# Pool waits tile by tile, the first mLSTM inputs on GpSimd's queue, and modulation tiles behind cells and evacuations

## The chip, the cores and the metric

The kernel runs on one core of one Trainium2 chip. The metric is the device time of one execution in microseconds. Three executions of the kernel before took 1891.66, 1893.18 and 1893.83 us; the median is 1893.18.

## The reference

One layer of a diffusion trunk is computed in float32 for 128 context tokens and 512 latent tokens, 640 in all, with a model width of 1024:

```python
def layer(x, mods, l, p, ctx):
    hh = rmsnorm(x, g[0]) * (1 + m[1]) + m[0]
    x = x + 0.5 * m[2] * swiglu(hh, p['ffn1_w1'][l], p['ffn1_w3'][l], p['ffn1_w2'][l])
    hh = rmsnorm(x, g[1]) * (1 + m[4]) + m[3]
    y, ctx_out = token_mixer(hh, p, l, ctx)
    x = x + m[5] * y
    hh = rmsnorm(x, g[2]) * (1 + m[7]) + m[6]
    x = x + 0.5 * m[8] * swiglu(hh, p['ffn2_w1'][l], p['ffn2_w3'][l], p['ffn2_w2'][l])
...
def token_mixer(h, p, l, ctx):
    mq, mk, mv, mo, mg, dq, dk, dv, gm, gd = split_cols(h @ p['w_in'][l])
    ...
    att = diff_attention(q_att, keys, vals, lam)
    ...
    h_f, st_f = mlstm_chunkwise(q, k, v, log_i[0], log_f[0], st0_f)
    h_b, st_b = mlstm_chunkwise(rev(q), rev(k), rev(v), ...)
    hm = (h_f + rev(h_b)).transpose(0, 2, 1, 3)
    hm = (rmsnorm(hm, p['g_mh'][l]).reshape(B, T, ML_WIDTH) * jax.nn.sigmoid(mo))
    y = jax.nn.sigmoid(gm) * (hm @ p['w_br_m'][l]) + jax.nn.sigmoid(gd) * (att @ p['w_br_d'][l])
    out = y @ p['w_out'][l]
```

The nine modulation vectors `m[j]` are columns of `silu(c) @ w_ada + b`. The attention has 8 heads, the mLSTM 4 heads of 256, in 5 chunks of 128 tokens and two directions; its state `C` starts at zero for the context chunk and from an input for the latent chunks.

## The kernel before, in words

Activations lie feature by feature: a tile holds 128 features by 640 tokens. A product of full precision is made of three matmuls on halves: a weight tile `raw` (128x2048, 1 MB) is cast by ScalarE (ACT) to a high part `wH` (L123), VectorE (DVE) subtracts to make the low part `wL` (L39, from `split_into`), and TensorE (PE) multiplies wH and wL with the high and low parts of the activations (`hH`/`hL` or `aHL`). A unit of such a product is 24 matmuls of 128x320 into one PSUM tile `ps_p`, followed by an evacuation; a granule is the four units of one weight tile.

The program runs through five stages: the first feed-forward; attention with the projections, interleaved; the mLSTM; the two branch products; the output product with the second feed-forward. The change touches the third and fourth, and the pools from the second on.

**Pools.** A `tile_pool` takes a stretch of SBUF or PSUM, and a later pool may take the same stretch. By default, the first tile of the later pool waits for everything that lay in the stretch. With `reuse_waits="tile"` each tile waits for what lay at its own addresses.

**mLSTM.** `Memory.load` fetches, per head, `va` (values, 640 KB), two halves of `P` (stabilisers, 320 KB each, one per direction, to which DVE adds `mask`), and `load_c` the two states `C`. `prep` makes token-major keys `mktok` (ACT, from PE's transposes), takes the exponentials of P on ACT (ten of 128x128 a head) and multiplies P by the scores `ps_st` on DVE. `cell` then does the chunk's products on PE (`ps_n`, `ps_u`), scales values to `wv`, updates `C` (or `Cn` for the context), and ends with `reciprocal` of `den` and, where the second direction is added, with `hs`. `gate` fetches `so` and applies a logarithm and an exponential to it (L1650, L1651 of the code below). `finish` normalises and transposes `hs` and multiplies it into `so`. Head h+1 is loaded and prepared among the cells of head h. Projections for the branch gates (evacuated to `stage` and written to `gm_dram`, `gd_dram`) and, at head 3, the splits of the attention output into `aHL` from `a_raw` stand between the cells.

**Branches.** Four granules of `w_brd` multiply `aHL`; `d_evac` multiplies a unit by a sigmoid `sig` into `y1`. Head 3's `finish` and the split of `zT_dram` (tiles `z_raw`, three at a time) into `hH`/`hL` stand among them. Four granules of `w_brm` then multiply those, and `m_evac` adds y1 and splits the sum into `yH` and `yL`. `x` comes back from `x_dram` by four transfers of 640 KB for the residual.

**Modulation tiles.** 23 of the columns of the modulation are still to be made in these stages, by `Columns`: `fetch` loads a weight column `raw_a` (512 KB), `tile` runs two multiply-and-sum passes over it on DVE (L671, printed as ISA in the order; 128x1024 each) against `csil`.

**One ring for all.** Weight tiles, `a_raw`, `z_raw` and `raw_a` share the pool `rawp` under one tag with two buffers. A load takes one of the two and waits until what lay there has been read for the last time: by wL's subtraction for a weight, by the second pass for a `raw_a`, by the last hL for a `z_raw`.

**What sets the order.** PE runs in program order, and so do the loads made by `load` (L74), which SyncE (SP) issues. The other instructions are placed by a scheduler, engine by engine, and each engine and queue then runs its list from front to back: an instruction that waits holds up everything behind it. `tc.issue_after(x)` makes what is written inside stand behind x. Most loads are issued by SP; the queue of GpSimd (POOL) is otherwise used for the feed-forwards.

The splits share one line, L39, and all matmuls one line, L52 (`mm`), so the rows of the profile are told apart by the tiles' names.

Of the kernel before, what the change touches and what calls it, by code (L numbers as in the profile page):

```python
# [31 lines left out]
def tile_trunk(ctx: ExitStack, tc: tile.TileContext, a: dict):  # L32
# [977 lines left out]


    att = ExitStack()
    ap = att.enter_context(tc.tile_pool(name="att", bufs=1))
    psum = att.enter_context(tc.tile_pool(name="ps2", bufs=5, space=PSUM))
    ps_s = att.enter_context(tc.tile_pool(name="ps2s", bufs=1, space=PSUM))

    fill = Fill()

# [376 lines left out]
            nc.sync.dma_start(out=dst[:, 2 * g + mt, half(hf)], in_=t)  # L1395
        return f

    with tc.tile_pool(name="gates", bufs=1) as gt:
# [20 lines left out]
    k_pool = ctx.enter_context(tc.tile_pool(name="mlk", bufs=1, side="right"))  # L1419
    queries_of = ExitStack()  # L1420
    q_pool = queries_of.enter_context(tc.tile_pool(name="mlq", bufs=1, side="right"))
# [111 lines left out]


    cs = ExitStack()
    cs_p = cs.enter_context(tc.tile_pool(name="csil", bufs=1, side="right"))
    csil = cs_p.tile([128, 2, D], F32, name="csil")
    for v in range(2):
        nc.sync.dma_start(out=csil[:, v, :], in_=csil_dram[v].partition_broadcast(128))
# [6 lines left out]
    columns.place(23, csil, load_columns, 0)  # L1546

    ml = ExitStack()
    mp = ml.enter_context(tc.tile_pool(name="ml", bufs=1))
    psum = ml.enter_context(tc.tile_pool(name="ps3", bufs=8, space=PSUM))  # L1550
    mask = load(mp, [128, 2, 128], a["mask"], name="mask")

    fill.pace(1.4, 1)
    for g in range(1, 4):
# [4 lines left out]
    class Memory:  # L1559
# [4 lines left out]

        def load(self):
            h = self.h
            self.va = mp.tile([128, 5, 258], F32, tag="va", name="va", bufs=2)
            nc.sync.dma_start(out=self.va[:, :, 0:256], in_=v_dram[h])
            vec.memset(self.va[:, :, 256:257], 1.0)
            vec.memset(self.va[:, :, 257:258], 0.0)  # L1570
            self.P = mp.tile([128, 5, 2, 128], F32, tag="P", name="P", bufs=2)
            for d in range(2):
                nc.sync.dma_start(
                    out=self.P[:, :, d, :], in_=nm_dram[32 * d + h].partition_broadcast(128).rearrange("p (c t) -> p c t", c=5)
                )
                tt(vec, self.P[:, :, d, :], self.P[:, :, d, :], mask[:, d, None, :].to_broadcast([128, 5, 128]), ALU.add)
            self.ktok = mp.tile([128, 5, 256], F32, tag="ktok", name="mktok", bufs=2)
            self.hs = mp.tile([128, 5, 256], F32, tag="hs", name="hs", bufs=2)

        def load_c(self):  # L1580
            self.C = [load(mp, [128, 2, 258], a["c_aug"][d, self.h], tag=f"C{d}", name="C", bufs=2) for d in range(2)]

        def prep(self, i):

# [15 lines left out]
        def cell(self, i, d, accumulate, inter, update):  # L1600

            h = self.h
            hd = 4 * d + h
            va, hs, C = self.va, self.hs, self.C[d]
            p1 = psum.tile([128, 512], F32, tag="mm", name="ps_n1")
            p1 = p1[:, :258]
            mm(p1, self.P[:, i, d, :], va[:, i, :], start=True, stop=True)
            tok = slice(i * 128, (i + 1) * 128)
            num = p1
            if inter:  # L1610
                p2 = psum.tile([128, 512], F32, tag="mm", name="ps_n2")
                p2 = p2[:, :258]
                for dt in range(2):
                    mm(p2, mqT[h][:, dt, tok], C[:, dt, :], start=dt == 0, stop=dt == 1)
                num = mp.tile([128, 258], F32, tag="num", name="num", bufs=3)
                act(num, p2, AF.Copy, scale=cols[:, i, 2, hd : hd + 1])
                tt(vec, num, p1, num, ALU.add)
            if update:
                wv_ = mp.tile([128, 258], F32, tag="wv", name="wv", bufs=2)
                act(wv_, va[:, i, :], AF.Copy, scale=cols[:, i, 1, hd : hd + 1])  # L1620
                if inter:
                    new = mp.tile([128, 2, 258], F32, tag=f"C{d}", name="C", bufs=2)
                else:
                    new = mp.tile([128, 2, 258], F32, tag="N", name="Cn", bufs=1)
                for dt in range(2):
                    p3 = psum.tile([128, 512], F32, tag="mm", name="ps_u")
                    p3 = p3[:, :258]
                    mm(p3, self.ktok[:, i, dt * 128 : (dt + 1) * 128], wv_, start=True, stop=True)
                    if inter:
                        stt(new[:, dt, :], C[:, dt, :], decay[:, 32 * d + h, i : i + 1], p3, ALU.mult, ALU.add)  # L1630
                    else:
                        act(new[:, dt, :], p3, AF.Copy)
                if inter:
                    self.C[d] = new
                else:
                    nc.sync.dma_start(out=a["new_c"][d, h], in_=new)
            den = mp.tile([128, 1], F32, tag="den", name="den", bufs=4)
            ts(den, num[:, 256:257], cols[:, i, 3, hd : hd + 1], ALU.max)
            stt(den, num[:, 256:257], -1.0, den, ALU.mult, ALU.max)
            vec.reciprocal(den, den)  # L1640
            if accumulate:
                stt(hs[:, i, :], num[:, 0:256], den, hs[:, i, :], ALU.mult, ALU.add)
            else:
                act(hs[:, i, :], num[:, 0:256], AF.Copy, scale=den)

# [60 lines left out]
    for h in range(4):  # L1706
        m = mem[h]
        later = [[] for _ in range(10)]
        if h < 3:
            mem[h + 1].load()  # L1710
            for i in range(5):
                later[3 + i].append(lambda i=i: mem[h + 1].prep(i))
        if h > 0:
            for i in range(5):
                later[4 + i].append(lambda i=i: mem[h - 1].finish(i))
        if h == 3:
            for k in range(KT):
                later[2 + k].append(attended)
        later[9].append(m.gate)
        steps = [(s, 0, s >= 2, True, s < 3) if d == 0 else (3 - s, 1, s >= 2, True, s < 3) for s in range(4) for d in range(2)]  # L1720
        steps += [(4, d, d == 1, False, True) for d in range(2)]
        for st, then in zip(steps, later):
            if st[0] == 4 and st[1] == 0 and h < 3:
                mem[h + 1].load_c()
            m.cell(*st)
            for f in then:
                f()
            fill.slot(0)
            if len(box_ml) % 4 == 0:
                columns.fetch(1)  # L1730
            elif len(box_ml) % 4 == 2:
                columns.tile()
            box_ml.append(0)
        m.stats()
    fill.drain()
# [13 lines left out]
    def d_evac(g):  # L1749
        def f(p, mt, hf):  # L1750
            t = gate_of(gd_dram, g, mt, hf, pool=mp, tag=("ktok", "P", "va", "hs")[g], bufs=2)
            tt(vec, y1[g][:, mt, half(hf)], p, t, ALU.mult)
        return f

    for g in range(4):
# [1 line left out]
    for i in range(5):  # L1757
        fill.one()
        mem[3].finish(i)
        columns.fetch((i + 1) % 2)  # L1760
        if i % 2:
            columns.tile()
    for k in range(6):
        if k % 3 == 0:
            raw = load(rawp, [128, 3, T], zT_dram[:, k : k + 3, :], tag="raw", name="z_raw")
# [14 lines left out]

    psum = Banks(ctx.enter_context(tc.tile_pool(name="ps4", bufs=1, space=PSUM)))
    tmp = ctx.enter_context(tc.tile_pool(name="tmp", bufs=1))
    out = ExitStack()
    zp = out.enter_context(tc.tile_pool(name="yy", bufs=1))
    x_pairs = pairs("k", "x")
    x = [x_pairs[d // 2][:, d % 2, :] for d in range(KT)]
    with tc.tile_pool(name="gate", bufs=1) as gp:
        yH, yL = hh_tiles(zp)
        yHL = [(yH[:, k], yL[:, k]) for k in range(KT)]

        def m_evac(g):
            def f(p, mt, hf):
# [3 lines left out]
                tt(vec, t, t, y1[g][:, mt, cs], ALU.add)  # L1796
                d = 2 * g + mt
                act(yH[:, d, cs], t, AF.Copy)
                tt(vec, yL[:, d, cs], t, yH[:, d, cs].bitcast(F32), ALU.subtract)
            return f  # L1800

        for g in range(4):
# [2 lines left out]
            nc.sync.dma_start(out=x_pairs[g], in_=x_dram[:, 2 * g : 2 * g + 2, :])  # L1805
# [219 lines left out]
```

## Time and profile before

| what | value |
|---|---|
| median of three executions | 1893.18 us |
| the profiled execution | 1891.94 us |
| its span in the profile | 1890.2 us |
| mean granted clock of PE | 0.986 |
| busy: PE, DVE, ACT, POOL | 1816.4, 1299.5, 847.0, 32.9 us |

The span is 1.74 us shorter than the execution it belongs to, and the median is 1.24 us above that execution. A row of the timeline gives the start and duration in microseconds, engine, line, operation, written tile and read tiles; repeated instructions are drawn together (x10), and in brackets stands the idle time ahead of the first and what ended it. "SPq" is the queue of issues on SP: the duration of such a row is that of issuing, not of the transfer. A row of the chain of waits has start, duration and what the span's end waited for in it. Rows of windows have the busy time and the count of instructions of each engine, and then the granted clock of PE ("PEclk"), the share of DMA and its rate.

### The profile page before, as it was taken

The page shows a single profiled execution, that of the slowest core. Times are in us where ns is not written, and L with a number is a line of the kernel's source. Part 1 is how long each engine was busy: PE and PEld are TensorE (multiplying, and loading weights), DVE is VectorE, ACT ScalarE, POOL GpSimd, SP SyncE. Part 2 cuts the span into 40 slices and gives each one's busy share as a digit, 9 for nine tenths or more (in the row PEclk, how much of TensorE's full clock was granted, in tenths as well). Part 3 has the DMA queues.
Part 4 walks back from the last instruction along what each step waited for, and adds up shares of the span by engine and source line. Part 5 has one row for each costly group of instructions (what it writes and reads, how often), then busy time and mean ns, then how long its engine had stood idle before and what let it go on. Part 6 is the DMA issues. An engine that isn't in the chain of part 4 may idle for free.

```text
span 1890.2 us, 30782 instructions
## 1 busy us (share of the span) xinstructions
PE 1816.4 (96%) x12658; PEld 1778.2 (94%) x12658; DVE 1299.5 (69%) x2193; ACT 847.0 (45%) x1447; POOL 32.9 (2%) x51
## 2 busy tenths in 40 slices
PE   6999999999989999999999989999999899999989
PEld 4999999999889999999999978899899899999989
DVE  7888885575787665754745457757666778886575
ACT  5644453112553354543543455663336555554232
POOL 1000001100000000000000000000000000000000
PEclk9999999999999999999999989999999999999999
DMA  8344449953325222221221255554742435547952
GB/s 325 119 165 163 154 149 330 323 190 118 116 88 174 100 76 80 73 98 51 84 93 59 98 194 166 191 196 162 266 155 80 150 126 184 185 172 269 336 193 91
DMA packets 127438, 299.82 MB, mean 159 GB/s; under 512 B 9473, under 2 KB 90625, under 8 KB 114625
## 3 DMA queue, kind: packets, MB, share of 16 engines
q1 hardware_dynamic: 118642, 259.07, 39.3%
q0 software_dynamic: 8656, 38.80, 5.6%
q8 instruction: 99, 1.62, 0.3%
q14 instruction: 41, 0.34, 0.1%
HBM read 234.20 MB, written 63.63 MB: 158 GB/s over the span
## 4 chain that ended last, share of the span: by engine, by line
PE 79%; DVE 9%; DMA 7%; ACT 3%; issue 2%; SPq 0%; DVEq 0%; ACTq 0%
PE ps_f L52 41%; PE ps_p L52 17%; PE ps_t L52 11%; DMA raw_a<-in_w_ada_c 3%; PE sc L52 2%; PE ps_o L52 2%; DMA ada<-csil_dram 1%; PE ps_n L52 1%; DVE junk L671 1%; PE ps_wT L55 1%; DMA P<-nm_dram 1%; PE ps_qkT L55 1%; DVE raw_a L671 1%; PE ps_u L52 1%; DVE wL L39 1%
## 5 line engine op out<-in xcount | busy, mean ns | idle before, releaser
L52 PE MATMUL ps_f<-S,ww 128*128 128x320 f32 x1992 | 319.6, 310 | 4.4 <-ACT ww L267 2.7
L52 PEld LDWEIGHTS ps_f<-S,ww 128*128 128x128 f32 x1992 | 300.1, 189 | 5.0 <-ACT ww L267 3.0
L52 PE MATMUL ps_p<-hH,wH 128*128 128x320 f32 x864 | 275.6, 319 | 9.3 <-DVE y L39 4.7
L52 PE MATMUL ps_p<-hL,wH 128*128 128x320 f32 x864 | 269.3, 312 | 0.0
L52 PE MATMUL ps_p<-hH,wL 128*128 128x320 f32 x864 | 269.3, 312 | 0.0
L52 PE MATMUL ps_f<-hm,ww 128*128 128x320 f32 x1248 | 200.9, 314 | 9.2 <-ACT ww L267 5.6
L52 PEld LDWEIGHTS ps_f<-hm,ww 128*128 128x128 f32 x1248 | 190.4, 192 | 10.3 <-ACT ww L267 5.9
L52 PE MATMUL ps_t<-wH,hH 128*128 128x256 f32 x640 | 186.0, 291 | 0.9 <-DVE x L42 0.9
L52 PE MATMUL ps_t<-wH,hL 128*128 128x256 f32 x640 | 181.9, 284 | 0.0
L52 PE MATMUL ps_t<-wL,hH 128*128 128x256 f32 x640 | 181.9, 284 | 0.0
L39 DVE TENSOR_TENSOR ww<-raw,ww 128x2048 fp32r<-128x2048 f32 (+1 forms) x62 | 138.8, 2238 | 52.6 <-ACT ww L267 40.4
L52 PEld LDWEIGHTS ps_p<-hH,wH 128*128 128x128 f32 x864 | 164.5, 190 | 11.0 <-issue 4.9
L52 PEld LDWEIGHTS ps_p<-hL,wH 128*128 128x128 f32 x864 | 164.4, 190 | 0.5
L52 PEld LDWEIGHTS ps_p<-hH,wL 128*128 128x128 f32 x864 | 164.3, 190 | 0.0
L52 PE MATMUL ps_f<-hm,wB 128*128 128x320 f32 x1008 | 161.5, 309 | 0.0
L52 PEld LDWEIGHTS ps_f<-hm,wB 128*128 128x128 f32 x1008 | 151.3, 188 | 0.0
L267 ACT ACTIVATE ww<-raw 128x2048 fp32r<-128x2048 f32 x48 | 91.8, 1912 | 102.2 <-DVE raw L39 53.4
L39 DVE TENSOR_TENSOR wL<-raw,wH 128x2048 fp32r<-128x2048 f32 x49 | 112.0, 2287 | 34.9 <-ACT wH L123 34.9
L123 ACT ACTIVATE wH<-raw 128x2048 fp32r<-128x2048 f32 x49 | 93.6, 1910 | 92.8 <-PE ps_p L52 78.3
L52 PEld LDWEIGHTS ps_t<-wH,hH 128*128 128x128 f32 x640 | 123.7, 193 | 1.4 <-ACT hH L201 1.1
L39 DVE TENSOR_TENSOR raw<-raw 128x1024 f32<-128x1024 f32 (+1 forms) x144 | 123.9, 862 | 1.4
L52 PEld LDWEIGHTS ps_t<-wL,hH 128*128 128x128 f32 x640 | 123.7, 193 | 0.3 <-issue 0.2
(295 smaller groups left out, 3225.7 us busy)
## 6 DMA issues: line engine op xcount, KB each, us to landing
g_dram<-g SPq DMA_DIRECT2D x44, 640.0 KB, 4.3
raw_a<-in_w_ada_c SPq DMA_DIRECT2D x32, 512.0 KB, 4.3
raw<-in_w1b SPq DMA_DIRECT2D x11, 1024.0 KB, 4.8
raw<-in_w3b SPq DMA_DIRECT2D x11, 1024.0 KB, 4.9
raw<-in_w1a SPq DMA_DIRECT2D x10, 1024.0 KB, 5.0
raw<-in_w3a SPq DMA_DIRECT2D x10, 1024.0 KB, 4.8
hm<-g_dram POOLq DMA_DIRECT2D x8, 1280.0 KB, 10.0
raw_a<-in_w_ada_k SPq DMA_DIRECT2D x8, 1024.0 KB, 10.0
```

Of the source, the lines that this page charges most:

```text
L39: return eng.tensor_tensor(out=out, in0=in0, in1=in1, op=op)
L52: tc.keep_in_program_order(nc.tensor.matmul(*args, **kw))
L55: tc.keep_in_program_order(nc.tensor.transpose(*args, **kw))
L123: act(h, raw, AF.Copy)
L267: act(t[0], flat, AF.Copy)
L671: vec.tensor_tensor_reduce(out=junk, in0=raw, in1=self.csil[:, v, :], op0=ALU.mult, op1=ALU.add, scale=1.0, scalar=0.0, accum_out=mod[:, c ...
```

## The change

Four things are done.

1. The pools of the mixing and of what follows it (`att`, `ps2`, `ps2s`, `gates`, `mlk`, `mlq`, `csil`, `ml`, `ps3`, `ps4`, `tmp`, `yy`, `gate`, `out`) get `reuse_waits="tile"`.
2. `mask` and head 0's `va`, `P` (twice) and `C` (twice) are loaded by GpSimd's queue instead of SP's.
3. A modulation tile of the mLSTM stage stands behind the last cell's `at_vec` (its reciprocal, or its sum into `hs`), and one of the branch stage behind the last evacuation's write (`box["y"]`: `y1`, or `yL`).
4. In the branch stage, `columns.ahead` is 1, and the alternating fetch of one and two columns ahead is gone.

```diff
@@ from L1012, and likewise for gates, mlk, mlq, csil, ml, ps3, ps4, tmp, yy, gate, out
-    ap = att.enter_context(tc.tile_pool(name="att", bufs=1))
+    ap = att.enter_context(tc.tile_pool(name="att", bufs=1, reuse_waits="tile"))
...
-    mask = load(mp, [128, 2, 128], a["mask"], name="mask")
+    mask = mp.tile([128, 2, 128], F32, name="mask")
+    nc.gpsimd.dma_start(out=mask, in_=a["mask"])
...
         def load(self):
             h = self.h
+            queue = nc.sync if h else nc.gpsimd
             self.va = mp.tile([128, 5, 258], F32, tag="va", name="va", bufs=2)
-            nc.sync.dma_start(out=self.va[:, :, 0:256], in_=v_dram[h])
+            queue.dma_start(out=self.va[:, :, 0:256], in_=v_dram[h])
...
-                nc.sync.dma_start(
+                queue.dma_start(
                     out=self.P[:, :, d, :], in_=nm_dram[32 * d + h].partition_broadcast(128).rearrange("p (c t) -> p c t", c=5)
...
         def load_c(self):
-            self.C = [load(mp, [128, 2, 258], a["c_aug"][d, self.h], tag=f"C{d}", name="C", bufs=2) for d in range(2)]
+            self.C = [mp.tile([128, 2, 258], F32, tag=f"C{d}", name="C", bufs=2) for d in range(2)]
+            for d in range(2):
+                (nc.sync if self.h else nc.gpsimd).dma_start(out=self.C[d], in_=a["c_aug"][d, self.h])
...
-            vec.reciprocal(den, den)
+            self.at_vec = vec.reciprocal(den, den)
             if accumulate:
-                stt(hs[:, i, :], num[:, 0:256], den, hs[:, i, :], ALU.mult, ALU.add)
+                self.at_vec = stt(hs[:, i, :], num[:, 0:256], den, hs[:, i, :], ALU.mult, ALU.add)
...
             elif len(box_ml) % 4 == 2:
-                columns.tile()
+                columns.tile(m.at_vec)
...
-            tt(vec, y1[g][:, mt, half(hf)], p, t, ALU.mult)
+            box["y"] = tt(vec, y1[g][:, mt, half(hf)], p, t, ALU.mult)
...
         mem[3].finish(i)
-        columns.fetch((i + 1) % 2)
+        columns.ahead = 1
+        columns.fetch()
         if i % 2:
-            columns.tile()
+            columns.tile(box["y"])
...
         while fill.q:
-            columns.fetch((n + 1) % 2)
             fill.one()
             if n % 2 and columns.n:
-                columns.tile()
+                columns.tile(box["y"])
...
-                tt(vec, yL[:, d, cs], t, yH[:, d, cs].bitcast(F32), ALU.subtract)
+                box["y"] = tt(vec, yL[:, d, cs], t, yH[:, d, cs].bitcast(F32), ALU.subtract)
```

PE's list is the same before and now. The lists of ACT, DVE and SP differ from the end of attention on, and POOL's has six more loads. Three places are shown. A tile's number tells apart tiles of one name: P_11346 is head 0's, P_11479 head 1's.

**First place: ACT ahead of head 0's first cell.** Before:

```order
L1620 ACTIVATE wv_11494<-va_11342,cols_4600 128x258
L1620 ACTIVATE wv_11518<-va_11342,cols_4600 128x258
L1591 ACTIVATE mktok_11351<-ps_k_11455 128x256
L1591 ACTIVATE mktok_11351<-ps_k_11465 128x256
L1597 ACTIVATE P_11346<-P_11346,cols_4600 128x128 x10
L1616 ACTIVATE num_11491<-ps_n2_11488,cols_4600 128x258
L1597 ACTIVATE P_11479<-P_11479,cols_4600 128x128 x9
L1620 ACTIVATE wv_11540<-va_11342,cols_4600 128x258
L1597 ACTIVATE P_11479<-P_11479,cols_4600 128x128
L1650 ACTIVATE so_11832<-so_11832 128x1280
L1616 ACTIVATE num_11515<-ps_n2_11512,cols_4600 128x258
L1644 ACTIVATE hs_11352<-num_11491,den_11503 128x256
```

And now, from the same row on:

```order
L1595 ACTIVATE mktok_11351<-ps_k_11455 128x256
L1595 ACTIVATE mktok_11351<-ps_k_11465 128x256
L1601 ACTIVATE P_11479<-P_11479,cols_4600 128x128 x5
L1624 ACTIVATE wv_11494<-va_11342,cols_4600 128x258
L1624 ACTIVATE wv_11518<-va_11342,cols_4600 128x258
L1601 ACTIVATE P_11479<-P_11479,cols_4600 128x128 x5
L1654 ACTIVATE so_11832<-so_11832 128x1280
L1655 ACTIVATE so_11832<-so_11832 128x1280
L1601 ACTIVATE P_11346<-P_11346,cols_4600 128x128 x10
L1620 ACTIVATE num_11491<-ps_n2_11488,cols_4600 128x258
```

Head 1's ten exponentials and both passes over `so_11832` (L1654 and L1655 are the former L1650 and L1651) now stand ahead of head 0's ten, behind which they stood.

**Second place: SP's loads for the third granule of w_brd and the two z_raw.** Each row loads one tile; raw_a are modulation columns. Before:

```order
L1395 DMA gd_dram_4593<-stage_13210 128x320
L74 DMA raw_13384<-in_w_brd 128x2048
L74 DMA raw_a_13426<-in_w_ada_c 128x1024
L74 DMA z_raw_13428<-zT_dram_4589 128x1920
L74 DMA sig_13674<-gd_dram_4593 128x1280
L74 DMA z_raw_13436<-zT_dram_4589 128x1920
L74 DMA raw_a_13498<-in_w_ada_c 128x1024
```

Now:

```order
L74 DMA raw_a_13269<-in_w_ada_c 128x1024
L1395 DMA gd_dram_4593<-stage_13210 128x320
L74 DMA raw_a_13308<-in_w_ada_c 128x1024
L74 DMA raw_a_13382<-in_w_ada_c 128x1024
L74 DMA raw_13386<-in_w_brd 128x2048
L74 DMA sig_13674<-gd_dram_4593 128x1280
L74 DMA z_raw_13428<-zT_dram_4589 128x1920
L74 DMA z_raw_13436<-zT_dram_4589 128x1920
```

The third weight tile was raw_13384 and is now raw_13386. It took the buffer of the second weight tile (raw_13227, released by wL_13226), and now takes that of raw_a_13308, which is loaded ahead of it. z_raw_13428 took the buffer of raw_a_13426, which stood ahead of it, and now takes that of the third weight tile; z_raw_13436 took that of the third weight tile and now takes that of raw_a_13382.

DVE runs the passes that release those two columns here. Rows of L671 with a size of 128x1 write a pass's sum. Now:

```order
L39 TENSOR_TENSOR y1_13213<-ps_p_13231,sig_13256 128x320
L39 TENSOR_TENSOR y1_13213<-ps_p_13271,sig_13256 128x320
L39 TENSOR_TENSOR so_13131<-ps_hT_13298,so_13131 128x2x128
L39 TENSOR_TENSOR hL_13218<-so_13131,hH_13217 128x128
L671 ISA raw_a_13269,mod_90<-raw_a_13269,csil_11331 128x1024
L671 ISA mod_90 128x1
L39 TENSOR_TENSOR hL_13218<-so_13131,hH_13217 128x128
L671 ISA raw_a_13269,mod_90<-raw_a_13269,csil_11331 128x1024
L671 ISA mod_90 128x1
L39 TENSOR_TENSOR y1_13213<-ps_p_13310,sig_13256 128x320
L39 TENSOR_TENSOR so_13131<-ps_hT_13337,so_13131 128x2x128
L39 TENSOR_TENSOR hL_13218<-so_13131,hH_13217 128x128 x2
L39 TENSOR_TENSOR y1_13213<-ps_p_13345,sig_13256 128x320
L671 ISA raw_a_13308,mod_90<-raw_a_13308,csil_11331 128x1024
L671 ISA mod_90 128x1
L39 TENSOR_TENSOR so_13131<-ps_hT_13372,so_13131 128x2x128
```

The passes of raw_a_13269 and raw_a_13308 stand behind evacuations into y1_13213 and among head 3's so and hL; wL_13226, of the second weight tile, is two rows ahead of the first row shown.

**Third place: SP's loads of x and of the first two w_brm tiles** (raw_13791 and raw_13797). Before:

```order
L74 DMA raw_a_13680<-in_w_ada_c 128x1024
L74 DMA raw_a_13736<-in_w_ada_c 128x1024
L74 DMA raw_13791<-in_w_brm 128x2048
L74 DMA raw_13797<-in_w_brm 128x2048
L1805 DMA x_13776<-x_dram_94 128x1280
L1805 DMA x_13777<-x_dram_94 128x1280
L1805 DMA x_13778<-x_dram_94 128x1280
L1805 DMA x_13779<-x_dram_94 128x1280
```

Now:

```order
L74 DMA raw_a_13680<-in_w_ada_c 128x1024
L74 DMA raw_a_13736<-in_w_ada_c 128x1024
L1809 DMA x_13776<-x_dram_94 128x1280
L1809 DMA x_13777<-x_dram_94 128x1280
L1809 DMA x_13778<-x_dram_94 128x1280
L1809 DMA x_13779<-x_dram_94 128x1280
L74 DMA raw_13791<-in_w_brm 128x2048
```

The four loads of x moved from behind the two weight tiles to ahead of the first. raw_13791 takes the buffer of raw_a_13680 before and now.

More of the change, by code (lines that the diff above doesn't have):

```diff
@@ L1012, in tile_trunk @@
     att = ExitStack()
-    ap = att.enter_context(tc.tile_pool(name="att", bufs=1))
-    psum = att.enter_context(tc.tile_pool(name="ps2", bufs=5, space=PSUM))
-    ps_s = att.enter_context(tc.tile_pool(name="ps2s", bufs=1, space=PSUM))
+    ap = att.enter_context(tc.tile_pool(name="att", bufs=1, reuse_waits="tile"))
+    psum = att.enter_context(tc.tile_pool(name="ps2", bufs=5, space=PSUM, reuse_waits="tile"))
+    ps_s = att.enter_context(tc.tile_pool(name="ps2s", bufs=1, space=PSUM, reuse_waits="tile"))
     fill = Fill()
@@ L1396, in gate_evac @@
         return f
-    with tc.tile_pool(name="gates", bufs=1) as gt:
+    with tc.tile_pool(name="gates", bufs=1, reuse_waits="tile") as gt:
         src_v, e_v = project_v(0)
@@ L1417, in tile_trunk @@
         heads[0].scores(0)
-    k_pool = ctx.enter_context(tc.tile_pool(name="mlk", bufs=1, side="right"))
+    k_pool = ctx.enter_context(tc.tile_pool(name="mlk", bufs=1, side="right", reuse_waits="tile"))
     queries_of = ExitStack()
-    q_pool = queries_of.enter_context(tc.tile_pool(name="mlq", bufs=1, side="right"))
+    q_pool = queries_of.enter_context(tc.tile_pool(name="mlq", bufs=1, side="right", reuse_waits="tile"))
     def pair(tag, i, name):
@@ L1535, in tile_trunk @@
     cs = ExitStack()
-    cs_p = cs.enter_context(tc.tile_pool(name="csil", bufs=1, side="right"))
+    cs_p = cs.enter_context(tc.tile_pool(name="csil", bufs=1, side="right", reuse_waits="tile"))
     csil = cs_p.tile([128, 2, D], F32, name="csil")
@@ L1548, in tile_trunk @@
     ml = ExitStack()
-    mp = ml.enter_context(tc.tile_pool(name="ml", bufs=1))
-    psum = ml.enter_context(tc.tile_pool(name="ps3", bufs=8, space=PSUM))
-    mask = load(mp, [128, 2, 128], a["mask"], name="mask")
+    mp = ml.enter_context(tc.tile_pool(name="ml", bufs=1, reuse_waits="tile"))
+    psum = ml.enter_context(tc.tile_pool(name="ps3", bufs=8, space=PSUM, reuse_waits="tile"))
+    mask = mp.tile([128, 2, 128], F32, name="mask")
+    nc.gpsimd.dma_start(out=mask, in_=a["mask"])
     fill.pace(1.4, 1)
@@ L1779, in tile_trunk @@
     mix.close()
-    psum = Banks(ctx.enter_context(tc.tile_pool(name="ps4", bufs=1, space=PSUM)))
-    tmp = ctx.enter_context(tc.tile_pool(name="tmp", bufs=1))
+    psum = Banks(ctx.enter_context(tc.tile_pool(name="ps4", bufs=1, space=PSUM, reuse_waits="tile")))
+    tmp = ctx.enter_context(tc.tile_pool(name="tmp", bufs=1, reuse_waits="tile"))
     out = ExitStack()
-    zp = out.enter_context(tc.tile_pool(name="yy", bufs=1))
+    zp = out.enter_context(tc.tile_pool(name="yy", bufs=1, reuse_waits="tile"))
     x_pairs = pairs("k", "x")
     x = [x_pairs[d // 2][:, d % 2, :] for d in range(KT)]
-    with tc.tile_pool(name="gate", bufs=1) as gp:
+    with tc.tile_pool(name="gate", bufs=1, reuse_waits="tile") as gp:
         yH, yL = hh_tiles(zp)
@@ L1807, in tile_trunk @@
     cs.close()
-    fp = out.enter_context(tc.tile_pool(name="out", bufs=1))
+    fp = out.enter_context(tc.tile_pool(name="out", bufs=1, reuse_waits="tile"))
     class Halves:
```

## The prediction

> **What bounds the kernel now.** I read the page's busy shares and costliest groups first, then PE's waits in the part that the change reorders, then the chain of waits there.
>
> ```profile
> PE 1816.4 (96%) x12658; PEld 1778.2 (94%) x12658; DVE 1299.5 (69%) x2193; ACT 847.0 (45%) x1447; POOL 32.9 (2%) x51
> ...
> L39 DVE TENSOR_TENSOR wL<-raw,wH 128x2048 fp32r<-128x2048 f32 x49 | 112.0, 2287 | 34.9 <-ACT wH L123 34.9
> L123 ACT ACTIVATE wH<-raw 128x2048 fp32r<-128x2048 f32 x49 | 93.6, 1910 | 92.8 <-PE ps_p L52 78.3
> ```
>
> PE is busy for 96% of the span and its list is the same before and now, so the time changes only where PE's gaps change. A weight tile that has landed needs 1.91 us of cast and 2.29 us of subtraction, 4.2 us, before its low part can be used.
>
> The lists differ only from the end of attention on. PE's waits from 1095 to 1340 us (what it waited for, total, times, longest):
>
> ```profile
> PE ps_p L52 <- DVE y L39: 4.7, 1, 4.7
> PE ps_n L52 <- DVE P L39: 4.6, 1, 4.6
> ...
> PE ps_p L52 <- DVE wL L39: 1.2, 1, 1.2
> PE ps_n L52 <- ACT stage L1394: 1.2, 1, 1.2
> PE ps_n L52 <- ACT Cn L1632: 0.6, 1, 0.6
> PE ps_u L52 <- DVE C L42: 0.6, 1, 0.6
> ```
>
> Around the two longest, windows give busy times by engine, PE's granted clock, DMA share and rate:
>
> ```profile
> 1110.04:1116.87 6.83, 4.99 (x12) 3.97 (x13) 4.44 (x11) 4.48 (x16) 0.00 (x0) 0.50 1.10 368
> 1331.90:1338.73 6.83, 4.86 (x18) 4.89 (x19) 4.11 (x3) 1.91 (x1) 0.00 (x0) 0.50 1.01 417
> ```
>
> After each, PE ran at half clock for 6.83 us; its 4.86 us of work there would have taken 2.43 at full clock, so such a dip costs about 2.4 us beside the wait. The Trainium skill (TensorE: Matmul & The Clock Gate, Part 1: The HAM clock gate) says that an idle window of 3.4 us halves the clock and a busy one restores it; 6.83 us is two such windows, so the trace agrees.
>
> The wait for y at 1333.87 is the first w_brm product's. The chain runs through its weight:
>
> ```profile
> 1315.16 13.90 PE ps_p L52 x93
> ...
> 1331.03 1.86 DVE wL L39
> ...
> 1333.24 0.49 DVE y L39
> ...
> 1333.87 6.25 PE ps_p L52 x26
> ```
>
> All products of w_brd end at 1329.06. The weight's wL is written until about 1333.3 (1331.03 + 2.29), so y, the last write that the PSUM pool's first tile waits for, comes only 0.5 us behind the weight.
>
> **The change part by part.** The sum is made on the profiled execution, 1891.94 us; the median is 1.24 higher.
>
> *Up to 1095 us:* no list but POOL's differs. The six loads stand on a queue that has nothing else to do there; 1.9 MB more beside attention. I count 0, with bounds −0.9 (a load that starts earlier) and +2 (a write held up by them).
>
> *Head 0's first cell.*
>
> ```profile
> 1100.41 8.10 DMA P<-nm_dram
> ...
> 1108.60 0.84 DVE P L39
> ...
> 1109.46 1.87 ACT P L1597 x6
> ...
> 1111.88 2.92 PE ps_n L52 x6
> ```
>
> ```profile
> 1097.32 2.00 SPq L1539 DMA_DIRECT2D csil<-csil_dram  x2
> ...
> 1099.83 0.54 SPq L1568 DMA_DIRECT2D va<-v_dram  x1
> ```
>
> ```profile
> L1597 ACT ACTIVATE P<-P,cols 128x128 f32<-128x128 f32 x20 | 6.1, 387 | 0.5 <-DVE P L39 0.5
> L1620 ACT ACTIVATE wv<-va,cols 128x258 f32<-128x258 f32 x6 | 2.9, 502 | 1.6 <-DMA va<-v_dram 1.6
> ...
> L1650 ACT ACTIVATE so<-so 128x1280 f32<-128x1280 f32 x1 | 1.3, 1254 | 0.0
> ```
>
> Before, the last wait is P's transfer: landed 1108.5, mask added 1109.4, six exponentials (6.1/20 = 0.31 each) by 1111.33, one multiplication, PE at 1111.88. P now lands early. What is late next is ACT's place: head 0's exponentials stand behind ten of head 1, two wv and two passes over so (1.25 each). Head 1's P is now the next but one behind csil on SP: csil loses the wait that ended at 1097.3 (0.7 us), and va follows it, so P is issued about 1099.2, lands about 1106.9 (its second half 1108), and its mask is added by 1107.7 and 1108.8. ACT then does 10 × 0.31 + 0.9 + 2.5 = 6.5 us, to 1114.2, and six of head 0's to 1116.0; a multiplication of 0.44 and PE starts at 1116.5: **+4.6**. The dip stays. Bounds: −4.6 if ACT's order costs nothing, +6 if head 1's P or so lands 1.4 later.
>
> *Cells among 1186 and 1208.* The waits for stage, Cn and C (1.2 + 0.6 + 0.6 = 2.4) fall together with modulation passes and aHL ahead of them, which have moved behind the cells; one C now stands behind four sums into hs (0.48 each), about 1.1. **−1.3**, bounds −2.4 and +0.5.
>
> *Branch products of w_brd.*
>
> ```profile
> 1280.29 0.33 SPq L74 DMA_DIRECT2D raw<-in_w_brd  x1
> ```
>
> ```profile
> 1290.50 4.94 DMA z_raw<-zT_dram
> ...
> 1298.56 3.62 DMA raw_a<-in_w_ada_c
> ...
> 1312.91 2.21 DVE wL L39
> ```
>
> ```profile
> L671 DVE CUSTOM_DVE_ANT_0 raw_a<-raw_a,csil 128x1024 bf16<-128x1024 f32 x36 | 43.6, 1220 | 25.3 <-DMA raw_a<-in_w_ada_c 19.6 <-DMA csil<-csil_dram 5.6
> ...
> L39 DVE TENSOR_TENSOR so<-ps_hT,so 128x256 f32<-128x256 f32 x20 | 8.3, 414 | 1.7 <-PE ps_hT L55 1.7
> ...
> L39 DVE TENSOR_TENSOR y<-ps_p,sig 128x320 f32<-128x320 f32 x16 | 7.6, 484 | 0.0
> ...
> L39 DVE TENSOR_TENSOR hL<-z_raw,hH 128x640 fp32r<-128x640 f32 x6 | 4.8, 821 | 2.5 <-ACT hH L1766 2.5
> ...
> L39 DVE TENSOR_TENSOR hL<-so,hH 128x128 fp32r<-128x128 f32 x10 | 2.5, 287 | 0.5 <-ACT hH L1672 0.4
> ```
>
> The ring makes one chain of it. The third weight was issued at 1280.29, when the second's wL ended. It now waits for the second pass over raw_a_13308. From 1280.3 DVE has ahead of it four passes (4.9), four y (1.9), two so (0.8) and seven hL (2.0): 9.6, and about 2 of waits for ACT's hH: 1291.9. By transfers of 4.9 (w_brm's in the row below) it lands at 1296.8, and wL ends at 1301.1. Then z_raw_13428, issued 1290.50 before, takes its buffer at 1301.1 and z_raw_13436 that of raw_a_13382 at about 1304; with the 4.9 of the row, shorter where only one flows, the second lands at 1308.5, and a cast and three hL (0.75 + 2.5) end at 1311.8. This buffer goes to the fourth weight: landed 1316.8, cast 1318.7. On DVE a pass over raw_a_13563 stands ahead of its wL. That column is issued behind the second pass over raw_a_13498, at about 1315.1; with 3.6 of transfer and 1.2 of a pass wL starts at 1320 and ends at 1322.3. Before, PE got it at 1315.16: **+7.2**, in which lie smaller waits for the first and third weight (0.85 and 0.55 by the same reckoning). PE then waits 7 us at the fourth weight, which the 1.2 of before did not make a dip of and the two longer waits did: **+2.4**. Bounds: 0 (each of the moves covered) and +12 (another 2.4 of waits for ACT).
>
> *First product of w_brm.*
>
> ```profile
> 1324.32 3.96 SPq L74 DMA_DIRECT2D raw<-in_w_brm  x2
> 1328.33 2.11 SPq L1805 DMA_DIRECT2D x<-x_dram  x4
> ```
>
> ```profile
> raw<-in_w_brm SPq DMA_DIRECT2D x3, 1024.0 KB, 4.9
> ```
>
> Now x goes ahead, into places that aHL held. They are read for the last time in the first half of the last w_brd unit, which is 24 of the 93 matmuls ahead of 1329.06, 3.6 us; so x is issued from 1326.1 on, which I call t. SP gets to the weight at t + 2.5, when the column in its buffer is read too. At the 417 GB/s of the second window, a weight alone (1.05 MB, 2.5 us of flow) has 2.4 us of lead. Four x (2.62 MB) take 6.3 us: the weight has landed at t + 2.4 + 6.3 + 2.5 = t + 11.2, is cast at t + 13.1, and wL ends at t + 15.4. Before, PE came to the first matmul with wL 0.6 us behind 1333.87, t + 8.4: **+7.0**, bounds +5.5 (the two flow side by side) and +8.5. The dip is there already. The Trainium skill (DMA: Bandwidth & Descriptors, Queues, rings and completion order) says that a DMA engine takes the descriptors of a queue in ring order, by which the weight comes wholly behind x; no run here shows it yet, and sharing by halves would end the weight at an estimated t + 9.9 and the sum 1.3 lower.
>
> *Third and fourth w_brm weight.* Their loads too wait for columns behind evacuations now. A granule lasts 14 us (93 matmuls in 13.90), a load and its halves 4.9 + 4.2, so a buffer may come 5 us late at no cost; by the same reckoning each wL comes 0.8 late, and I take **+0.8** for both, bounds 0 and +3. The output product and the feed-forward keep their order.
>
> Sum: 4.6 − 1.3 + 9.6 + 7.0 + 0.8 = **+20.7**, 1912.6 on the profiled execution; with part of the 1.24 to the median, **1913**.
>
> **The rivals.**
> 1. *The w_brd weights are covered.* If the scheduler's column passes run earlier than I add up (the waits for hH), the ring frees its buffers 8 us earlier and PE sees none of it. For it: a granule's 14 us leave 5 us of slack to every buffer. Against: three places of the ring move the same way, the third weight by 11 us. 1891.94 + 4.6 − 1.3 + 7.0 = 1902.2.
> 2. *All branch weights are covered, or the passes' new places hold nothing up.* Then only the mLSTM terms are left: 1895.2, within 0.2%. Against: SP's list has x ahead of the weight, and x cannot start before the aHL are read.
> 3. *Faster: the pool's wait at 1333.87 goes, and the product starts at once.* It holds if the first w_brm weight is issued by 1320.1 (4.9 + 1.9 + 2.3 ahead of 1329.2), so that PE goes on without wait and dip: −4.7 − 2.4, and 1884.8. For it: y was the last thing PE waited for. Against: the weight itself was only 0.5 us earlier, and is now behind x, which waits until 1326.
>
> **How the numbers follow.** Forecast 0.70 (1903 to 1922 by the bounds of the terms, which do not all fall together), the first rival 0.12, the second 0.07, the third 0.11. The range takes in the first rival, 1899 to 1922, and leaves the other two out. About 0.2% (3.8 us) is what a measurement of this kernel can tell from no change: faster 0.11, same 0.07, slower 0.82.
>
> **What would show it.** The first ps_n at about 1116.5, with ACT at so and head 0's P just before. The third w_brd load issued near 1292, a wait of PE for wL of 7 to 8 us ahead of the fourth, and a window of clock 0.50 behind it. x issued ahead of the weight, and PE's wait for wL, not for y, of some 11 us at the first w_brm product. I am wrong if PE waits there for less than 5 us, or if the first cell starts before 1112.

## The result, and the profile after

The changed kernel takes 1918.18 us (median of 5 runs, 1915.33 to 1921.53) against 1891.66 us before (5 runs, 1889.98 to 1893.83): the ratio is 1.0136, 95% interval 1.0124 to 1.0148. It is slower by some 26 us. The forecast was 1913, with 1899 to 1922 as its range. The profiled execution of the changed kernel took 1917.38 us and spans 1915.6 us; before it was 1891.94 and 1890.2, so the two traces differ by 25.4 us.

The busy line of the page of the changed kernel, and its waits of PE from 1090 to 1370 us (total, times, longest):

```profile
PE 1820.9 (95%) x12658; PEld 1782.8 (93%) x12658; DVE 1303.1 (68%) x2193; ACT 846.9 (44%) x1447; POOL 37.1 (2%) x57
```

```profile
PE ps_p L52 <- ACT wH L123: 13.0, 3, 10.4
PE ps_n L52 <- issue: 10.2, 1, 10.2
PE ps_p L52 <- DVE wL L39: 6.9, 3, 3.7
PE ps_p L52 <- ACT aT L1324: 2.5, 1, 2.5
PE ps_n L52 <- DVE C L42: 1.3, 1, 1.3
PE ps_n L52 <- ACT Cn L1636: 1.2, 1, 1.2
PE ps_p L52 <- DVE C L42: 0.8, 1, 0.8
```

PE does the same 12658 matmuls. The wait for y at the first w_brm product is gone, as the change meant, and a wait of 10.4 for that product's weight stands there. The wait ahead of the first ps_n has grown from 4.6 to 10.2; "issue" means that the profile names no releaser, and the timeline of ACT below gives it. A wait of 3.7 for wL is new: it is the fourth w_brd weight's.

Since PE's list is the same in all these kernels, the k-th matmul of one trace can be set against the k-th of another. This table takes the start of the same matmul at eight places, subtracts the trace of before, and shows what each stage adds (us):

| stage, up to (start before) | predicted | changed | e4: parts 1, 2 | e3: parts 3, 4 | e7: cell tiles held | e9: branch tiles held | e5: x last |
|---|---|---|---|---|---|---|---|
| last ps_st of head 0 (1107.01) | 0 | 1.7 | -0.6 | -0.5 | 1.9 | -2.5 | 0.4 |
| first cells (1129.70) | 4.6 | 4.6 | 4.4 | -0.3 | 6.4 | 6.4 | 4.4 |
| cells (1207.24) | -1.3 | -1.7 | -1.6 | -2.0 | -2.8 | -1.2 | -1.5 |
| first w_brd product (1270.03) | 0 | 0.1 | -0.1 | -0.1 | -0.1 | 0.0 | -0.1 |
| end of w_brd (1328.89) | 9.6 | 11.3 | 0.4 | 9.5 | 9.5 | 8.0 | 11.7 |
| in the first w_brm granule (1352.28) | 7.0 | 7.0 | 0.6 | 7.2 | -5.2 | 8.4 | 3.1 |
| end of w_brm (1416.81) | 0.8 | 2.5 | 0.0 | 2.5 | 0.0 | 2.2 | 4.8 |
| end (1886.25) | 0 | 0.2 | 0.5 | 0.1 | -0.9 | -1.0 | -1.3 |
| sum | 20.7 | 25.5 | 3.5 | 16.4 | 8.7 | 20.3 | 21.5 |

The first row varies by −2.5 to +1.9 among kernels whose lists agree there but for POOL's loads (e3's agree wholly), and in the trace of e1, whose lists are those of before, the row of the cells is +2.1. So no row is read closer than by some 2 us.

**First cell.** ACT of the changed kernel:

```profile
1110.57 1.57 ACT L1601 ACTIVATE P<-P,cols 128x128 f32<-128x128 f32 x5 [1.63 <-DVE P L39]
1112.05 0.89 ACT L1624 ACTIVATE wv<-va,cols 128x258 f32<-128x258 f32 x2
1112.85 1.55 ACT L1601 ACTIVATE P<-P,cols 128x128 f32<-128x128 f32 x5
1114.31 1.25 ACT L1654 ACTIVATE so<-so 128x1280 f32<-128x1280 f32 x1
1115.59 1.27 ACT L1655 ACTIVATE so<-so 128x1280 f32<-128x1280 f32 x1
1116.77 3.01 ACT L1601 ACTIVATE P<-P,cols 128x128 f32<-128x128 f32 x10
```

And DVE, which adds mask to both halves of both heads at one go, once head 1's P is there:

```profile
1109.71 3.26 DVE L39 TENSOR_TENSOR P<-P,mask 128x640 f32<-128x640 f32 x4 [11.75 <-DMA P<-nm_dram]
```

On ACT, head 1's ten exponentials and both passes of so run first, and head 0's ten, which the first product needs, begin at 1116.77. PE starts at 1119.17.

**Branch products.** The chain of waits of the changed kernel:

```profile
1297.94 4.74 DMA raw<-in_w_brd
...
1307.03 4.61 DMA z_raw<-zT_dram
...
1321.62 3.75 DMA raw_a<-in_w_ada_c
...
1326.74 2.21 DVE wL L39
...
1329.00 12.64 PE ps_p L52 x70
...
1341.66 0.49 DVE y L39
1342.15 1.13 DVE raw_a L671
1343.33 1.22 DVE raw_a L671
1344.59 8.92 DMA raw<-in_w_brm
...
1353.61 1.92 ACT wH L123
1355.55 2.30 DVE wL L39
...
1357.90 17.17 PE ps_p L52 x106
```

The third w_brd weight, the z_raw, a column and the fourth weight follow each other through the ring. The first w_brm weight is issued when the second pass behind a y has freed its buffer, and takes 8.92 us behind x, which SP issued ahead of it:

```profile
1342.10 2.03 SPq L1809 DMA_DIRECT2D x<-x_dram  x4
```

The windows of the dips, that is of the stretches at half clock (granted clock third from the end). Three stand behind the three long waits; the one at 1279.02 stands behind two waits, of 0.8 and 1.8 us, for the first w_brd weight:

```profile
1111.77:1122.01 10.24, 2.84 (x7) 2.31 (x8) 2.95 (x7) 7.98 (x21) 0.00 (x0) 0.50 0.02 6
1279.02:1282.43 3.41, 3.41 (x15) 3.41 (x14) 0.00 (x0) 3.38 (x4) 0.00 (x0) 0.50 1.03 408
1326.81:1333.64 6.83, 4.64 (x17) 4.64 (x18) 3.63 (x5) 0.00 (x0) 0.00 (x0) 0.50 0.42 140
1347.29:1360.94 13.65, 3.94 (x13) 3.54 (x14) 2.29 (x1) 4.32 (x3) 0.00 (x0) 0.50 0.77 307
```

### The profile page after: what moved, and what is told of

Same layout as the page of the kernel before. It is cut to its first block, busy times and chain, and to the rows that moved or that the text cites. A ratio compares the mean times of both kernels' runs of the same rounds, so it can differ in the third digit from the quotient of the medians.

```text
span 1915.6 us, 30767 instructions
## 1 busy us (share of the span) xinstructions
PE 1820.9 (95%) x12658; PEld 1782.8 (93%) x12658; DVE 1303.1 (68%) x2193; ACT 846.9 (44%) x1447; POOL 37.1 (2%) x57
## 4 chain that ended last, share of the span: by engine, by line
PE 77%; DVE 10%; DMA 8%; ACT 3%; issue 2%; SPq 0%; DVEq 0%; ACTq 0%
PE ps_f L52 40%; PE ps_p L52 16%; PE ps_t L52 11%; DMA raw_a<-in_w_ada_c 2%; PE sc L52 2%; PE ps_o L52 2%; DMA ada<-csil_dram 1%; PE ps_n L52 1%; DVE junk L671 1%; PE ps_wT L55 1%; DVE wL L39 1%; DVE raw_a L671 1%; PE ps_qkT L55 1%; DMA P<-nm_dram 1%; PE ps_u L52 1%
## 5 line engine op out<-in xcount | busy, mean ns | idle before, releaser
L52 PE MATMUL ps_p<-hH,wH 128*128 128x320 f32 x864 | 275.6, 319 | 14.2 <-ACT wH L123 10.4
L52 PEld LDWEIGHTS ps_p<-hH,wH 128*128 128x128 f32 x864 | 164.3, 190 | 15.8 <-ACT wH L123 10.7
```

The costliest lines, as they stand in the source:

```text
L52: tc.keep_in_program_order(nc.tensor.matmul(*args, **kw))
```

## The experiments

Every run was set against runs of the kernel before on the same chip (medians 1892.1 to 1893.9 us).

**e1: part 1 alone**, the fourteen pools of the kernel before:

```diff
-    psum = Banks(ctx.enter_context(tc.tile_pool(name="ps4", bufs=1, space=PSUM)))
+    psum = Banks(ctx.enter_context(tc.tile_pool(name="ps4", bufs=1, space=PSUM, reuse_waits="tile")))
```

> The kernel before with only part 1: reuse_waits on the fourteen pools. The lists of all engines are those of before, so this prices the pool waits alone. Theory of the prediction: the waits by tile move nothing by themselves; csil may start 0.7 us earlier and the first w_brm product at most 0.5 us (y behind the weight's low part): 0 to -1.2 us against before. Rival (the removed waits are what costs, since early transfers collide with others): slower by 5 us or more. Rival (the wait for y at the first w_brm product was worth its 4.7 us and a dip): faster by 5 to 7 us.

Measured 0.9996 (0.9988 to 1.0005): no change. In its waits of PE, the 4.7 for y have become waits for the weight's two parts:

```profile
PE ps_p L52 <- DVE wL L39: 2.6, 2, 1.8
...
PE ps_p L52 <- ACT wH L123: 2.5, 1, 2.5
```

PE came to the first w_brm product 2.2 us sooner and gave it back at its third matmul, the first with wL. The pool's wait was covered by the weight, and its removal is worth nothing by itself.

**e2: part 2 alone**, with `queue = nc.sync if h else nc.gpsimd` and mask and C likewise, and the pools as before.

> The kernel before with only part 2: mask and head 0's five loads on GpSimd's queue. Theory: ACT's list puts head 1's ten exponentials and so's two passes ahead of head 0's ten, as in the changed kernel, so the first cell starts 4 to 6 us later: +4 to +6 us against before, with a wait of some 9 to 11 us ahead of the first ps_n. Rival (the first cell's lateness comes from the waits by tile or from the modulation tiles): 0 to +1 us here.

Measured 1.0050 (1.0037 to 1.0064), some 9.5 us: worse than either theory had it. PE's wait, and POOL's issue of P in this run:

```profile
PE ps_n L52 <- DVE P L39: 16.0, 1, 16.0
```

```profile
1100.28 1.73 POOL L1575 DMA_DIRECT2D P<-nm_dram  x2
```

Here the loads still wait for the pool: P is issued at 1100.28, no sooner than SP did it. Head 1's loads run beside head 0's, and DVE adds mask only when they have landed:

```profile
1114.91 3.27 DVE L39 TENSOR_TENSOR P<-P,mask 128x640 f32<-128x640 f32 x4 [5.56 <-DMA P<-nm_dram]
```

The loss of ACT's order comes on top.

**e3: parts 3 and 4 alone**, `columns.tile(m.at_vec)`, `columns.tile(box["y"])` and `columns.ahead = 1` in the kernel before.

> The kernel before with only parts 3 and 4: modulation tiles behind cells and evacuations, one column ahead. Theory: all that was lost in the branch products is here, without the first cell's loss: w_brd +9 to +11, first w_brm +6 to +7, later w_brm +1 to +2, mLSTM -1 to 0: +16 to +20 us against before, with waits for the fourth w_brd weight and of about 10 us for the first w_brm weight. Rival (the loss needs the waits by tile as well, which let x start early): +9 to +12 us only.

Measured 1.0088 (1.0074 to 1.0101), 16.7 us. The first cell is unharmed, and the wait for the first w_brm weight is there without tile-wise pools:

```profile
PE ps_p L52 <- ACT wH L123: 14.2, 2, 10.5
```

SP issues x ahead of that weight here too (1332.77 and 1335.27). In e4 and e7, which leave the branch tiles free, x is issued behind both weights. So the place of x comes with parts 3 and 4, not with the pools.

**e4: parts 1 and 2**, the changed kernel without 3 and 4.

> The changed kernel without parts 3 and 4: waits by tile and GpSimd's queue only. Theory: the first cell's loss remains and the branch stage is that of before: +4 to +6 us against before, so 20 us faster than the changed kernel. Rival (parts 1 and 2 together are free, the whole loss is that of parts 3 and 4): 0 to +1. Rival (parts act together, not as a sum): more than +8.

Measured 1.0021 (1.0011 to 1.0032), 4.0 us; in the table the first cell alone has 4.4. Against e2, waits by tile let POOL issue P 25 us sooner, and halve the loss:

```profile
1075.56 1.73 POOL L1575 DMA_DIRECT2D P<-nm_dram  x2 [51.71 <-PE sc L52]
```

e3 and e4 add up to 20.7 us of the 25.7 (1.36% of 1892), with intervals of about 2 us each. In the traces, from the second row of the table on, they add 16.9 and 4.1 and the changed kernel 23.8; 1.4 of the difference is in w_brd.

**e5: x behind the first two w_brm weights** in the changed kernel:

```diff
+        fill.prefetch(0)
+        fill.prefetch(1)
+        with tc.issue_after(last[0].ins):
             for g in range(4):
                 nc.sync.dma_start(out=x_pairs[g], in_=x_dram[:, 2 * g : 2 * g + 2, :])
```

`last[0]` is the last load issued by `dma`.

> The changed kernel with the four loads of x issued behind the first two w_brm weights (their old place); all else as changed. In the changed kernel's trace the first w_brm weight is issued at 1344.6, when the modulation pass behind the last y1 evacuation but one has released its buffer, and takes 8.9 us to land behind x. Theory now: x ahead is 4 of the 7 us there, the late release the rest: 3 to 5 us faster than the changed kernel, +1.1% against before, with the weight landing in about 5 us. The prediction as it stood (x ahead is all of it): 7 us faster. Rival (the transfer is slow for another reason, such as other transfers): no change, the weight still lands in 8 to 9 us.

Measured 1.0108 (1.0094 to 1.0123): about 5 us faster than the changed kernel's 1.0136. The chain of this run:

```profile
1340.60 0.49 DVE y L39
...
1342.26 1.23 DVE raw_a L673
...
1343.52 4.72 DMA raw<-in_w_brm
```

The weight lands in 4.72 us in place of 8.92: that 4.2 is x's. Its issue still waits for the two passes behind y. In the table 3.9 of the 7.0 go at the first w_brm product, and 2.3 more are lost at the later ones, where a dip of 3.41 us follows the wait for the fourth weight.

**e6: head 0 first** in the changed kernel: head 1's mask additions and head 0's so passes behind head 0's own P:

```diff
+                    if h == 1:
+                        st.enter_context(tc.issue_after(mem[0].at_p.ins))
                     tt(vec, self.P[:, :, d, :], self.P[:, :, d, :], mask[...], ALU.add)
...
+                if h == 0:
+                    st.enter_context(tc.issue_after(mem[0].at_e.ins))
                 act(self.so, self.so, AF.Ln, bias=1.0)
```

`at_e` is head 0's last exponential, `at_p` its last multiplication.

> The changed kernel with head 1's mask additions on DVE, and its so passes on ACT, put behind head 0's (head 1's exponentials then follow); all else as changed. Theory: head 0's P is there early, so the first cell starts about 9 us sooner, within 1 us of the end of the last ps_st: 8 to 12 us faster than the changed kernel (9.5 us of wait and up to 2.5 of half clock). Rival (the early loads themselves are late or slow): the wait ahead of the first ps_n stays above 5 us. Rival (the time is given back when head 1's P comes later): the first cell is sooner, the total within 3 us of the changed kernel.

Measured 1.0100 (1.0086 to 1.0114), about 7 us faster than the changed kernel: less than the 8 to 12 expected. PE's wait ahead of the first ps_n fell from 10.2 to 3.1:

```profile
1110.05 0.90 ACT L1627 ACTIVATE wv<-va,cols 128x258 f32<-128x258 f32 x2
1110.85 3.01 ACT L1604 ACTIVATE P<-P,cols 128x128 f32<-128x128 f32 x10
```

P had its mask long before (DVE at 1100.6 and 1101.4), but ACT's list has head 0's exponentials behind five mktok and two wv, so they begin at 1110.85. Of the 7.1 us of wait, 1.5 are lost again: the dip has 5.8 us of PE's work in it, in place of 2.84. In the trace the first cells are 1.1 us ahead of before, where the changed kernel lost 4.6. The run moves rows on DVE and on ACT together, and does not tell the two apart.

**e7: branch tiles free**, those of the mLSTM stage still behind their cells.

> The changed kernel with the modulation tiles of the branch stage (those behind y1 and yL) set free and fetched as before; those of the mLSTM stage stay behind their cells. Theory: the branch stage is that of before again, the first cell keeps its loss, and the mLSTM tiles behind cells are worth -1 to 0: +3 to +5 us against before, 20 us faster than the changed kernel. Rival (tiles behind cells push later work into the branch stage, so that much of the loss stays): +8 or more.

Measured 1.0043 (1.0031 to 1.0055), 8.1 us: the rival. The w_brd products lose 9.5 us although the branch tiles are free again; 5.2 come back at w_brm, whose first weight is issued 7 us ahead of the end of w_brd (1343.75 in this trace). PE waits 2.6 us for the first w_brd weight, with a dip of 3.41 behind it, and 3.3 for the fourth. In the chain the first w_brd weight is late, as in the changed kernel:

```profile
1269.41 5.13 DMA raw<-in_w_brd
...
1336.78 4.78 DMA raw<-in_w_brm
```

Before, by SP's timeline, the first w_brd weight was issued 39 us sooner:

```profile
1230.89 0.42 SPq L74 DMA_DIRECT2D raw<-in_w_brd  x1
```

**e8: parts 1 and 2, and head 0 first**, no tiles held.

> Parts 1 and 2 without the modulation tiles' places, and head 0's P first on DVE and ACT. Theory: the loss of the first cell turns into the gain that early loads allow: before waited 4.6 us there and ran 6.8 us at half clock, so 3 to 6 us faster than before. Rival (early loads are worth nothing because the start of the first cell is bound elsewhere, by ps_st or wv): within 1 us of before.

Measured 0.9991 (0.9981 to 1.0000): 1.7 us, with an interval of 0 to 3.6, nearer to the rival's size than to the theory's. The wait at the first ps_n is 6.5 us here, on account of DVE:

```profile
1109.72 1.22 DVE L671 CUSTOM_DVE_ANT_0 raw_a<-raw_a,csil 128x1024 bf16<-128x1024 f32 x1
...
1110.87 1.56 DVE L39 TENSOR_TENSOR P<-P,mask 128x640 f32<-128x640 f32 x2
```

Four modulation passes, which wait for csil, stand ahead of head 0's mask additions. This is what holding the tiles behind cells avoids in e6, where the additions ran ten microseconds sooner.

**e9: mLSTM tiles free**, those of the branch stage still behind y1 and yL.

> The changed kernel with the modulation tiles of the mLSTM stage set free; those of the branch stage stay behind y1 and yL. It asks what made the four w_brd weights late. Theory A (the prediction: the branch tiles' passes hold the ring's buffers): the w_brd loss of 8 to 11 us stays; +22 to +24 us against before. Theory B (the tiles held behind cells, since the run with only those still lost 9 us in w_brd: they leave the ring late, so the first w_brd weight comes 1269 instead of 1231): the w_brd loss falls to 0 to 4 us, while the w_brm loss of about 7 and the first cell's of 4.5 stay; +13 to +17 us against before.

Measured 1.0123 (1.0108 to 1.0137), 23.3 us: theory A. PE's waits in the branch products are near those of the changed kernel, but it does not wait for the first w_brd weight, and for the fourth it waits 7.2 us (3.7 for its high part, 3.5 for its low):

```profile
PE ps_p L52 <- ACT wH L123: 14.3, 2, 10.6
...
PE ps_p L52 <- DVE wL L39: 6.5, 4, 3.5
```

So either set of held tiles alone makes w_brd 8 to 9.5 us late, and both together 11.3. They reach PE in different places: the cell tiles alone (e7) at the first and the fourth weight, the branch tiles alone (e9) at the fourth. The branch tiles were held only together with part 4, so that no run tells these two apart.

**e10: e8 with the w_brm granules queued ahead of the w_brd drain**, so that the first w_brm weight is fetched when the fourth w_brd product begins:

```diff
+    for g in range(4):
+        fill.granule(a["w_brm"][g], lambda g=g: feat_units(psum, box["m_evac"](g), zHL))
-    def drain_beside_columns():
+    def drain_beside_columns(leave=0):
         n = 0
-        while fill.q:
+        while len(fill.q) > leave:
...
-    drain_beside_columns()
+    drain_beside_columns(4)
     ml.close()
```

> The kernel of the eighth run (parts 1 and 2, head 0 first, no tiles held) with the w_brm granules queued ahead of the w_brd drain, so that the first w_brm weight is loaded three modulation columns earlier, when the fourth w_brd product begins. Theory: the first w_brm product was bound by its weight (issue, 4.9 us, cast, low part), not by the pool: its wait of about 5 us and the dip of clock go, 5 to 8 us faster than before. Rival (the wait is y's, the pool's or the modulation columns' and only moves): within 2 us of the eighth run.

Measured 1885.72 us against 1893.69: 0.9961 (0.9947 to 0.9975), some 7 us faster than before and the fastest of all. Its trace does not show where these come from. It is that of the slowest of its six executions (1890.24 us), and its span of 1888.4 is only 1.8 shorter than that of before. In it the first w_brm product comes 6.8 us sooner against the end of w_brd, and 4.3 are lost at the second weight, which is issued at 1332.74 in place of 1327.95; PE waits for it and a dip of 3.41 us follows. Between 1290 and 1400 PE waits:

```profile
PE ps_p L52 <- DVE wL L39: 2.3, 2, 1.8
PE ps_p L52 <- ACT wH L123: 0.4, 1, 0.4
```

Set against e8's trace, the branch products gain 1.2 us in all, the rival's size, while the medians give nearly 6, the theory's. Which of them holds stays open.

**e11: the same queueing in the kernel before**, and **e12: with part 1 as well.**

> The kernel before, with only the w_brm granules queued early: pool waits as they were. Theory: the weight is there, and the pool's wait for the last y is laid bare: a wait of 0.6 to 1.2 us at the first w_brm product, in place of 4.7 and a dip; 4 to 7 us faster than before. Rival (the pool wait is worth several us, since the later products' low parts queue behind it): a wait above 2 us there.

> Part 1 and the early w_brm weight: the same as the eleventh run, with waits by tile. Theory: the wait of 0.6 to 1.2 us at the first w_brm product is gone, 0.5 to 1.5 us faster than the eleventh run; the time alone may not tell it, the trace does. Rival: PE waits there all the same, for sig or for the second part of the weight.

e11 measured 1.0004 (0.9994 to 1.0014), no change; e12 0.9987 (0.9978 to 0.9995). In e11's chain the weight is ready, and PE waits 5.3 us for y:

```profile
1327.42 2.30 DVE wL L39
...
1329.74 3.79 DMA raw_a<-in_w_ada_c
...
1333.55 1.23 DVE raw_a L671
...
1336.33 0.41 DVE y L39
...
1336.88 8.26 PE ps_p L52 x42
```

The evacuations stand behind a modulation pass that waits for its column, which could be fetched only when wL had freed the buffer. So the expected 0.6 to 1.2 us was wrong: y is held too, by the weight's own ring. In e12 PE still waited 4.0 us, for a y and not, as the rival had it, for sig or the weight; in e10 it did not wait there, with the same rows on DVE; presumably the first tile's bank is another unit's there, which was not looked into.

## Why the prediction came out right, point by point

- **Up to 1095 us.** 0 was predicted; the trace shows 1.7, but other kernels' traces scatter by as much there. It is not shown to be the change's.
- **First cell, +4.6.** Measured 4.6 (4.4 in e4). The path was right, but the number is two misses that cancel. The first ps_n starts at 1119.17, which is 1117.5 without the 1.7, where 1116.5 was predicted: PE's wait is 5.6 us longer than before. The first half of head 1's P took 9.8 us from its issue to its landing, where the step reckons with 7.7, and ACT's rows follow from there. The dip stayed, as predicted, but it holds 2.84 us of PE's work in place of 4.99, so that an estimated 1.1 us less is lost in it. That head 1's rows ahead of head 0's are the cause is shown by e6: with head 0's rows first the whole loss is gone.
- **Cells, −1.3.** Measured −1.7, but the step failed: its number came out by luck. The waits that were to fall from 2.4 to 1.1 (stage, Cn and C from 1186 on) are 2.5 in the changed kernel, 1.2 for Cn and 1.3 for C. About 1.0 was gained at another wait, at 1156.93 before, which the step left out:

```profile
PE ps_p L52 <- ACT num L1616: 1.8, 1, 1.8
```

That wait is 0.8 now, for a C. And e4, which holds no tiles behind cells, has −1.6 in this row.

- **w_brd, +9.6.** Measured 11.3. Taking off the 4.7 us by which the trace is late when w_brd begins, the third weight's load is at 1293.3 (predicted 1291.9), the first z_raw at 1302.4 (1301.1), and the fourth weight's wL ends at 1324.3 (1322.3). This chain was right, and 1 to 2 us short from its first link on. PE's waits were shared out otherwise. The sign, a wait of 7 to 8 us for wL at the fourth weight, did not come: PE waited 1.8 us for wH and 3.7 for wL there. The term that was too small is the first weight's, 0.85 without a dip. PE waited 2.5 us for it, and the dip at 1279.02 cost an estimated 1.7 more. It was issued at 1268.65, and at 1230.89 before; e7 has the same lateness and e9 does not, so it comes from the mLSTM tiles, which the step did not see.
- **First w_brm product, +7.0.** Measured 7.0. Its clock t, the first issue of x, is 1342.1: 1326.1 and the 16.0 by which the trace is late there. (The prediction's own figures, 1329.06 and 3.6, give 1325.5; the 0.6 more is not worked out, but came out.) The weight was issued at t + 2.5, landed at t + 11.4 and its wL ended at t + 15.8, against 2.5, 11.2 and 15.4. The landings also decide what was left open about the queue: the last of the four x landed at 1351.0 and the weight 2.5 us behind it, the time of its own flow, while sharing by halves would have given t + 9.9. The Trainium skill (DMA: Bandwidth & Descriptors, Queues, rings and completion order) says that an engine takes descriptors in ring order. The trace agrees. e5 then splits the step. By the step's own terms a weight issued at t + 2.5 without x has its wL ready at t + 11.6 (4.9 + 1.9 + 2.3 behind its issue), 3.2 us later than PE came to it before; e5 lost 3.1. So x has some 3.9 of the 7.0, and the late release of the buffer the rest.
- **Later w_brm weights, +0.8.** Measured 2.5, inside its bounds of 0 to 3: PE waited 0.5 us for the third weight and 1.4 for the fourth. The lateness of each weight was set too small, as in w_brd.
- **The sum.** 20.7 against 25.5: 1.7 for w_brd, 1.7 for the later weights and 1.7 ahead of the first cell, less 0.4 for the cells. The branch products have 20.8 of the 25.5, and there the path was the predicted one but for the first w_brd weight. The close agreement of the first cell and of the cells is no evidence for their sizes.
- **The rivals.** That the branch weights are covered is excluded by the table. The faster case, that the pool's wait at 1333.87 was worth its 4.7 us and a dip, is excluded by e1 (no change). Whether the place was worth something with the weight early is open: by the medians e10, with the weight early, the waits by tile and the first cell's order mended, gains 7 us, and e1, e11 and e12, with one or two of these, gain 0 to 2.5; but e10's trace does not show it.

## What to carry to other kernels

A wait that a profile names as last may have a second one half a microsecond behind it: here the pool's wait (e1) and the weight's load (e11) were both worth nothing alone, and 2.5 us together (e12). Before work is pushed behind a milestone, look at which ring buffer it holds and who loads into that buffer next; the delay then runs on through a load, a cast and a subtraction (4.7, 1.9 and 2.3 us here), and is not the length of the work moved. And when a load is made earlier, read what a scheduler puts ahead of its consumers: head 0's P landed some 24 us sooner, and ACT took it up 7 us later.

## What was not expected of the hardware

The length of a dip does not tell its price. The four dips of the changed kernel shown above lasted 10.24, 3.41, 6.83 and 13.65 us, all multiples of 3.41. At a clock of 0.50, matmuls of 128x320 start every 0.27 us, and every 0.15 behind the last dip's end. So a dip costs about half of PE's busy time in it, by estimate 1.4, 1.7, 2.3 and 2.0 us. The longest is twice as long as the one at the same place before, which holds 4.86 us of work and cost 2.4. It cost less all the same, since most of it lies in waits, of 10.4 us for wH and 1.4 for wL.

Nor does a dip need one long wait. The one at 1279.02 stands behind waits of 0.8 and 1.8 us, and cost two thirds of what they did. The idle window of 3.4 us, by which the prediction reads its dips, does not cover it.
